# Second layer's output projection: where its weights are loaded, cast and split

## The chip, the cores and the metric

The kernel runs on one core of a Trainium2 chip. A core has five engines with an instruction queue each: TensorE (PE in the profile, its weight loads PEld), VectorE (DVE), ScalarE (ACT), GpSimd (POOL) and SyncE (SP), which here only starts transfers. Each engine takes its instructions strictly in the order in which the program put them; an instruction that waits for a semaphore holds up everything behind it on its engine. Sixteen DMA engines carry the transfers that SP and POOL start. The metric is the device time of one execution in microseconds, the median over several executions.

## The reference

Two pre-norm residual layers over 1024 tokens of width 1024, and a last RMS norm. The first layer is a gated linear recurrence, the second is causal attention with a forget gate, 16 heads of width 64. Of the second layer the change touches the last line alone, the product with `fox_w_out`.

```python
def fox_mixer(h, w_in, b_f, w_out):
    ...
        logits = jnp.einsum("bqhd,bkhd->bhqk", q_blk.astype(jnp.float32), kf) * scale
        logits = logits + (cq_blk[..., :, None] - ck[:, :, None, :])
        ...
        p = jax.nn.softmax(logits, axis=-1)
        return jnp.einsum("bhqk,bkhd->bqhd", p, vf)
    ...
    y = o * jax.nn.silu(gate)
    return y @ w_out.astype(h.dtype)
...
        x = x + fox_mixer(h, fox_w_in[j], fox_b_f[j], fox_w_out[j])
    return rms_norm(x, final_g)
```

## The kernel before

Everything is held feature-major: a tile is 128 features by 512 tokens, one half of the sequence. float32 products are made of three: an operand is split into a high part in the short format of TensorE and a low part, the rest, and high*high, low*high and high*low are added up. The high part of a weight is a cast on ACT (`to_hi`, a CAST `wh<-wf` in the rows), the low part a subtraction on DVE that needs the cast's result (`to_lo`, L110, `wl<-wf,wh`). A weight tile comes from HBM into a buffer `wf`, of which there are three, in turn; `fetch` (L65) starts the load on SP's queue.

The attention goes head by head. For a head `hd` and a half `c` of its queries, `maxima` (L941) makes the scores `S` on TensorE in blocks of 128 queries, a maximum over the masked scores on DVE (L965), the exponential `p` on ACT with its row sums, the reciprocal of the sums and the split probabilities `pp` (ACT, then DVE L979), and a transpose of these by DMA on SP's queue into `pT` (L982). `weigh` (L988) then multiplies `pT` with the values `V` into `O`, `gated` and `split_y` make the layer's result `y` of it.

`run` (L1038) weaves these together by a string of digits: each digit takes one step of `weigh` or `maxima`, each dot one step of `fill`, independent TensorE work. For the heads 12 to 15 `fill` ends in `partial` (L1104). It walks over 16 tiles (db, c), db of the 8 blocks of 128 output features, c of the two halves, in the order (0,0), (1,0), (0,1), (1,1), (2,0), (2,1), (3,0) ... (7,1). A tile adds 18 products (six pairs of heads, three products each) in a bank `ops1`, adds the residual `x` that POOL's queue brought (L1113, L1116), and for most tiles POOL's queue writes it back. "Tile n" below means block db = n; both halves use the same weights. The last two pairs of heads come later (`late`, weights `woh`, `wol`; `turned`, bank `turn`), and the output follows from there.

The weights of block db are made by `split_out(db)` (L1084), with six blocks of 128x128 in two loads, one of 128x512 (256 KB) and one of 128x256 (128 KB), two casts and two subtractions. `partial` calls it at the head of a tile, for the tile itself if that is still to do, and for the next block where `c if db < 2 else not c` holds. So the program text puts load, cast and split of block db+1 ahead of a tile's products: those of block 2 ahead of the products of (1,1), those of block 3 ahead of (2,0), and so on.

The text is not the final order: the framework's scheduler places each instruction on its engine by priority, which follows the text, and by when its operands are expected. `tc.issue_after(x)` gives what stands under it a priority behind the instruction x. `seen[0]` is the exponential that was written last.

Of the kernel before, what the change touches and what calls it, by code (L numbers as in the profile page):

```python
# [12 lines left out]
F32R = mybir.dt.float32r  # L13
# [6 lines left out]
P = 128  # L20
SEQ = 1024
HALF = 512
KT = 8
# [12 lines left out]
def f32(ap):  # L36
    return ap.bitcast(F32)
# [3 lines left out]
def trunk(ctx: ExitStack, tc: tile.TileContext, xt, w0, wg, wo0, pc, gn, gf, w1, wv, wf, bf, wo1, out):  # L41
    nc = tc.nc

    def pool(name, bufs, **kw):
        return tc.tile_pool(name=name, bufs=bufs, **kw)
# [4 lines left out]
    wpool = ctx.enter_context(pool("w", 4))  # L50
# [14 lines left out]
    def fetch(to, src):  # L65
        loaded_last[0] = loads_by[0].dma_start(to, src)

    def matmul(*args, **kw):
        pe[0] = nc.tensor.matmul(*args, **kw)  # L69
        return pe[0]  # L70
# [25 lines left out]
    def to_hi(hi, src, eng, scale=None):  # L96
        if eng is nc.scalar:
            if scale is None:
                cast_last[0] = nc.scalar.copy(hi, src)
            else:  # L100
                nc.scalar.activation(hi, src, AF.Copy, scale=scale)
        elif eng is nc.gpsimd:
            nc.gpsimd.tensor_scalar(hi, src, 1.0 if scale is None else scale, 0.0, ALU.mult, ALU.add)
        elif scale is None:
            eng.tensor_copy(hi, src)
        else:
            eng.tensor_scalar(hi, src, scale, None, ALU.mult)

    def to_lo(lo, src, hi, eng):
        return eng.tensor_tensor(lo, src, f32(hi), ALU.subtract)  # L110
# [3 lines left out]
    def loaded(shape):  # L114

        if spare and next(loads) % 4 == 3:
            return spare[0].tile([P, *shape], F32, tag="wx", name="wf")
        return wpool.tile([P, *shape], F32, tag="wf", name="wf", bufs=3)

    def split_weights(src, shape, hi_eng, lo_eng, parts=wpool):  # L120
        wt = loaded(shape)
        for part, sl in src:
            fetch(wt[:, :, sl], part)
        hi = parts.tile([P, *shape], F32R, tag="wh", name="wh")
        lo = parts.tile([P, *shape], F32R, tag="wl", name="wl")
        a, b, c = (t.rearrange("p a b -> p (a b)") for t in (wt, hi, lo))
        to_hi(b, a, hi_eng)
        to_lo(c, a, b, lo_eng)
        return [(hi[:, k], lo[:, k]) for k in range(shape[0])]

    def weights(src, parts=wpool, lo_eng=nc.gpsimd):

        for k in range(0, src.shape[1], 4):
            n = min(4, src.shape[1] - k)
            yield from split_weights([(src[:, k : k + n], slice(0, P))], (n, P), nc.scalar, lo_eng, parts)

    def gemm_steps(ps, pairs, chunks=(slice(0, HALF),)):

        pairs = list(pairs)
        for cs in chunks:  # L140
            o = ps[:, cs]
            for i, ((wh, wl), (xh, xl)) in enumerate(pairs):
                matmul(o, wh, xh[:, cs], start=i == 0, stop=False)
                matmul(o, wl, xh[:, cs], start=False, stop=False)
                matmul(o, wh, xl[:, cs], start=False, stop=i == len(pairs) - 1)
                if i % 2:
                    yield
# [51 lines left out]
    with nullcontext(ExitStack()) as l0:  # L199
# [45 lines left out]
        k = 0  # L245
# [138 lines left out]
        def out_weights(g, d0):  # L384

            wt = loaded([4, P])
            for j in range(2):
                nc.sync.dma_start(wt[:, 2 * j : 2 * j + 2], wo0[d0 + j, :, 2 * g : 2 * g + 2])
            hi = wpool.tile([P, 4, P], F32R, tag="wh", name="wh")
            lo = wpool.tile([P, 4, P], F32R, tag="wl", name="wl")  # L390
            to_hi(hi, wt, nc.scalar)
            to_lo(lo, wt, hi, nc.vector)
            return [[(hi[:, 2 * j + i], lo[:, 2 * j + i]) for i in range(2)] for j in range(2)]
# [184 lines left out]
        wl = [w for d0 in range(0, KT, 2) for w in out_weights(NB // 2 - 1, d0)]  # L578
# [41 lines left out]
    with ExitStack() as l1:  # L620
# [11 lines left out]
        seen = [None]  # L632
# [137 lines left out]
        wo = {}  # L770
# [306 lines left out]
        def beside(steps, first, more):  # L1077

            for i, _ in enumerate(steps):
                if i >= first:  # L1080
                    next(more, None)
                yield

        def split_out(db):  # L1084
            if db < KT and db not in wo:
                wo[db] = list(weights(wo1[db, :, :6], lo_eng=nc.vector))

        def first_out():
            split_out(0)
            yield from ()  # L1090
# [3 lines left out]
        def home(db):  # L1094

            if db == 4:
                two = at.tile([P, 2, HALF], F32, tag="sg", name="x3")
                homes[4], homes[3] = two[:, 0], two[:, 1]
            elif db == 5:
                four = tu.tile([P, 4, HALF], F32, tag="T0", name="x4")  # L1100
                homes.update(zip((2, 5, 6, 7), (four[:, i] for i in range(4))))
            return homes[db]

        def partial(todo):  # L1104

            for db, c in todo:
                split_out(db)
                if c if db < 2 else not c:
                    split_out(db + 1)

                kept = c == 0 and db > 3
                x = home(db) if kept else rpool.tile([P, HALF], F32, tag="R", name="xp")
                nc.gpsimd.dma_start(x, x1d[c, :, db])  # L1113
                pt = ps.tile([P, HALF], F32, tag="g", name="ops1")
                yield from gemm_steps(pt, zip(wo[db], [y1[c][pair] for pair in range(6)]))
                nc.vector.tensor_tensor(x, x, pt, ALU.add)  # L1116
                if not kept:
                    nc.gpsimd.dma_start(x1d[c, :, db], x)
# [135 lines left out]
        for hd in range(HEADS):  # L1254
            pair = hd // 2
            if hd % 2 == 0:
                if hd < 12:
                    fill = play(next(fills))
                elif hd == 12:
                    todo = [(db, c) for c in range(2) for db in range(2)]  # L1260
                    todo += [(db, c) for db in range(2, KT) for c in range(2)]
                    splits = [split_loaded(c) for c in range(2)]
                    fill = chain(
                        play(next(fills)),
                        play(last_g[0]),
                        high_y(0),
                        first_out(),
                        beside(play(last_g[1]), 1, splits[0]),
                        high_y(1),
                        beside(partial(todo), 3, splits[1]),  # L1270
                        last_gains(),
                        turned(0, 0),
                        turned(0, 1),
                    )
            elif pair < 6:
                fill = play(next(fills))
# [86 lines left out]
def build(arrays):  # L1363
    import concourse.bacc as bacc

    nc = bacc.Bacc("TRN2", target_bir_lowering=False, num_devices=1)
    args = [
        nc.dram_tensor(f"in_{k}", v.shape, mybir.dt.from_np(v.dtype), kind="ExternalInput").ap()
        for k, v in arrays.items()
    ]  # L1370
    args.append(nc.dram_tensor("out_t", (KT, P, SEQ), F32, kind="ExternalOutput").ap())
    with tile.TileContext(nc, schedule_with_timeline_sim=True) as tc:
        trunk(tc, *args)
    return nc
# [9 lines left out]
```

## Time and profile before

| | |
|---|---|
| three runs | 1059.81, 1063.55, 1062.22 us; median 1062.22 |
| the profiled execution, its own time | 1059.12 us |
| its span, first to last instruction | 1057.4 us |
| mean granted TensorE clock | 0.996 |
| DMA | 148.92 MB, of it 161937 of 219806 packets under 512 B |
| `wf<-in_wo` | 64 loads of 128 KB on average, SP's queue |

The heads 12 to 15, and with them `partial`, run from about 928 us (the first product of `ops1`) to 1018 us; the end of the program follows. A row of the timeline gives start, length, engine, line, operation, output<-input and form, and in brackets how long the engine was idle before it and what ended that. SPq is SP's queue; its rows give the time that starting a transfer took, not its arrival. The names in the rows have no buffer numbers.

### The profile page before, as it was taken

To read this page: it belongs to the slowest core of one execution; us is meant where nothing else is said; L and a number is where in the kernel's file an instruction comes from. 1 tells how busy PE (TensorE), PEld (TensorE's weight loads), DVE (VectorE), ACT (ScalarE), POOL (GpSimd) and SP (SyncE) were. 2 spreads that over 40 slices of the span, in tenths; PEclk is the share of its full clock that TensorE was granted. 3 is DMA by queue.
4 is the path that set the end of the run, shared out by engine and by line. 5 is a ranking of instruction groups with operands and counts; after the bars stand their busy time and mean duration, and the time that the engine had idled before them with its cause. 6 is when DMAs were issued, how large, how long until landed. Compare 5 with 4: busy or idle time off the path is not lost. (4 is left out here: it accounts for less than half of the span.)

```text
span 1057.4 us, 15071 instructions
## 1 busy us (share of the span) xinstructions
PE 1022.6 (97%) x5094; PEld 710.3 (67%) x5094; DVE 786.5 (74%) x1456; ACT 660.7 (62%) x1211; POOL 90.6 (9%) x87
## 2 busy tenths in 40 slices
PE   9999999999999999998999989999999999999997
PEld 6787878888888888765444456444754448477676
DVE  7789657667856868895879875888578875986575
ACT  8479666565657565567656755666466764854455
POOL 1311112012101120001000000000000000012100
PEclk9999999999999999999999999999999999999999
DMA  7112424233423311443688993898748985789984
GB/s 246 61 50 63 124 84 144 68 115 108 133 66 113 122 50 48 161 141 75 150 166 169 185 208 70 182 192 175 182 95 189 176 190 133 168 196 250 230 199 160
DMA packets 219806, 148.92 MB, mean 141 GB/s; under 512 B 161937, under 2 KB 174865, under 8 KB 219729
## 3 DMA queue, kind: packets, MB, share of 16 engines
q1 hardware_dynamic: 217328, 140.09, 54.0%
q0 software_dynamic: 2400, 7.87, 2.5%
q8 instruction: 40, 0.66, 0.2%
q14 instruction: 38, 0.30, 0.1%
HBM read 73.33 MB, written 11.67 MB: 80 GB/s over the span
## 5 line engine op out<-in xcount | busy, mean ns | idle before, releaser
L69 PE MATMUL gps<-h,w 128*128 128x512 f16 x1152 | 269.1, 380 | 1.3 <-DVE qkl L795 1.1
L69 PEld LDWEIGHTS <-w 128*128 128x128 f16 x1152 | 104.2, 98 | 126.8 <-issue 14.0
L57 ACT ACTIVATE p<-S,m 128x128 f32<-128x128 f32 (+7 forms) x128 | 94.4, 738 | 78.0 <-DVE m L965 32.4
L57 ACT ACTIVATE pp<-p,sums 128x128 f16<-128x128 f32 (+7 forms) x128 | 96.6, 770 | 34.9 <-DVE sums L977 22.0
L979 DVE SCALAR_TENSOR_TENSOR pp<-p,sums,pp 128x128 f16<-128x128 f32 (+7 forms) x128 | 102.5, 812 | 13.5 <-ACT pp L57 12.4
L69 PE MATMUL S<-T,U 96*128 96x512 f32 (+7 forms) x384 | 106.4, 386 | 5.2 <-ACT p L57 4.1
L965 DVE CUSTOM_DVE_ANT_0 S<-S,mask 128x128 f32<-128x128 f32 (+7 forms) x128 | 96.9, 758 | 11.8 <-PE S L69 10.5
L69 PE MATMUL vps<-w,h 128*128 128x256 f16 (+1 forms) x768 | 90.6, 280 | 11.4 <-ACT w L57 7.4
L110 POOL TENSOR_TENSOR wl<-wf,wh 128x512 fp32r<-128x512 f32 x46 | 69.3, 1511 | 324.5 <-ACT wh L57 268.5
L69 PEld LDWEIGHTS <-h 128*128 128x128 f16 x768 | 76.3, 100 | 25.9 <-issue 9.9
L69 PEld LDWEIGHTS S<-T,U 128*128 128x128 f32 (+1 forms) x384 | 66.9, 189 | 39.3 <-ACT p L57 19.1
L57 ACT CAST wh<-wf 128x512 fp32r<-128x512 f32 x88 | 51.6, 592 | 51.1 <-PE ops L69 27.6
L69 PE MATMUL ups<-hh,wh 128*128 128x512 f32 x192 | 76.2, 398 | 1.1 <-ACT hh L57 1.0
L69 PE MATMUL ops<-yh,wh 128*128 128x512 f32 x192 | 76.7, 399 | 0.6 <-ACT yh L57 0.6
L69 PE MATMUL ups<-hh,wl 128*128 128x512 f32 x192 | 75.7, 394 | 1.0 <-POOL wl L110 1.0
L69 PE MATMUL ups<-hl,wh 128*128 128x512 f32 x192 | 76.2, 397 | 0.2
L69 PE MATMUL ops<-yh,wl 128*128 128x512 f32 x192 | 75.7, 394 | 0.1
L69 PE MATMUL gps<-hh,wh 128*128 128x512 f32 x192 | 75.7, 394 | 0.1
L69 PE MATMUL gps<-hh,wl 128*128 128x512 f32 x192 | 75.5, 393 | 0.0
L69 PE MATMUL gps<-hl,wh 128*128 128x512 f32 x192 | 75.5, 393 | 0.0
L403 DVE TENSOR_TENSOR x<-x,ops 128x512 f32<-128x512 f32 x80 | 54.0, 679 | 28.2 <-PE ops L69 27.9
L69 PE MATMUL ops<-yl,wh 128*128 128x512 f32 x192 | 74.6, 394 | 0.0
(196 smaller groups left out, 1877.9 us busy)
## 6 DMA issues: line engine op xcount, KB each, us to landing
wf<-in_w SPq DMA_DIRECT2D x106, 256.0 KB
wsf<-in_w SPq DMA_DIRECT2D x48, 256.0 KB
wf<-in_wo SPq DMA_DIRECT2D x64, 128.0 KB
T<-qkh SPq DMA_DIRECT2D x64, 128.0 KB
U<-qkh SPq DMA_DIRECT2D x64, 128.0 KB
x<-in_xt SPq DMA_DIRECT2D x16, 256.0 KB
wsf<-in_wv SPq DMA_DIRECT2D x16, 256.0 KB
x1d<-x SPq DMA_DIRECT2D x16, 256.0 KB
```

Source lines behind the costliest of these rows:

```text
L57: act[0] = op(*args, **kw)
L69: pe[0] = nc.tensor.matmul(*args, **kw)
L110: return eng.tensor_tensor(lo, src, f32(hi), ALU.subtract)
L403: nc.vector.tensor_tensor(x, x, pt, ALU.add)
L965: nc.vector.tensor_tensor_reduce(S[:, :n], S[:, :n], mask[:, SEQ - n :], -1.0, -NEG, ALU.add, ALU.min, accum_out=m)
L979: nc.vector.scalar_tensor_tensor(both[:, :, 1], p, r, both[:, :, 0], ALU.mult, ALU.subtract)
```

## The change

Load and split come apart. A new `load_out(db)` starts the two loads of a block; `split_out` calls it and then only casts and subtracts. `partial` loads the next block ahead of a tile's products, as before, but casts and splits it behind them, under `issue_after` of the exponential that was written last.

```diff
+        raw_out = {}
+
+        def load_out(db):
+            if db < KT and db not in raw_out:
+                raw_out[db] = []
+                for k, n in ((0, 4), (4, 2)):
+                    wt = loaded((n, P))
+                    fetch(wt, wo1[db, :, k : k + n])
+                    raw_out[db].append(wt)
+
         def split_out(db):
+            load_out(db)
             if db < KT and db not in wo:
-                wo[db] = list(weights(wo1[db, :, :6], lo_eng=nc.vector))
+                wo[db] = []
+                for wt in raw_out[db]:
+                    hi, lo = (wpool.tile([P, *wt.shape[1:]], F32R, tag=t, name=t) for t in ("wh", "wl"))
+                    to_hi(hi, wt, nc.scalar)
+                    to_lo(lo, wt, hi, nc.vector)
+                    wo[db] += [(hi[:, k], lo[:, k]) for k in range(wt.shape[1])]
...
                 split_out(db)
-                if c if db < 2 else not c:
-                    split_out(db + 1)
+                ahead = c if db < 2 else not c
+                if ahead:
+                    load_out(db + 1)
...
                 yield from gemm_steps(pt, zip(wo[db], [y1[c][pair] for pair in range(6)]))
+                if ahead:
+                    with tc.issue_after(seen[0].ins):
+                        split_out(db + 1)
                 nc.vector.tensor_tensor(x, x, pt, ALU.add)
```

TensorE's order does not change at all. On the other engines it does from the middle of `partial` on. The numbers in the names belong to one build each: block 2 is `wh_9049`, `wh_9055` before and `wh_9104`, `wh_9108` now.

ACT, where head 13 turns to head 14; before:

```order
L57 ACTIVATE p_8987,sums_8644<-S_8980,m_8985 128x1024
L57 CAST wh_9049<-wf_9047 128x512
L57 ACTIVATE pp_8989<-p_8987,sums_8644 128x8x128
L57 CAST wh_9055<-wf_9053 128x256
L57 ACTIVATE yo_8622<-O_9012,wsq_238 64x512
L57 ACTIVATE p_9037,sums_9030<-S_9032,m_9035 128x128
L57 CAST wh_9116<-wf_9114 128x512
L57 ACTIVATE pp_9039<-p_9037,sums_9030 128x128
L57 ACTIVATE p_9083,sums_9030<-S_9078,m_9081 128x256
L57 ACTIVATE pp_9085<-p_9083,sums_9030 128x2x128
L57 ACTIVATE p_9104,sums_9030<-S_9099,m_9102 128x384
L57 ACTIVATE pp_9106<-p_9104,sums_9030 128x3x128
```

and now:

```order
L57 ACTIVATE p_8987,sums_8644<-S_8980,m_8985 128x1024
L57 ACTIVATE pp_8989<-p_8987,sums_8644 128x8x128
L57 ACTIVATE yo_8622<-O_9012,wsq_238 64x512
L57 ACTIVATE p_9037,sums_9030<-S_9032,m_9035 128x128
L57 ACTIVATE pp_9039<-p_9037,sums_9030 128x128
L57 ACTIVATE p_9075,sums_9030<-S_9070,m_9073 128x256
L57 ACTIVATE pp_9077<-p_9075,sums_9030 128x2x128
L57 ACTIVATE p_9096,sums_9030<-S_9091,m_9094 128x384
L57 CAST wh_9104<-wf_9047 128x512
L57 CAST wh_9108<-wf_9049 128x256
L57 ACTIVATE pp_9098<-p_9096,sums_9030 128x3x128
```

The casts of block 2 moved from behind the exponential of 128x1024 to behind that of 128x384; the cast of block 3 left this stretch for a later place.

DVE, the same place, now (before, no `wl` stands between these two additions):

```order
L1136 TENSOR_TENSOR xp_9051<-xp_9051,ops1_9053 128x512
L965 ISA S_9091,m_9094<-S_9091,mask_4069 128x384
L965 ISA m_9094 128x1
L979 SCALAR_TENSOR_TENSOR pp_9077<-p_9075,sums_9030,pp_9077 128x2x128
L976 TENSOR_SCALAR sums_9030<-sums_9030 128x1
L977 RECIPROCAL sums_9030<-sums_9030 128x1
L110 TENSOR_TENSOR wl_9105<-wf_9047,wh_9104 128x512
L110 TENSOR_TENSOR wl_9109<-wf_9049,wh_9108 128x256
L979 SCALAR_TENSOR_TENSOR pp_9098<-p_9096,sums_9030,pp_9098 128x3x128
L965 ISA S_9135,m_9138<-S_9135,mask_4069 128x512
L965 ISA m_9138 128x1
L1136 TENSOR_TENSOR xp_9118<-xp_9118,ops1_9120 128x512
```

The two subtractions of block 2 moved behind the reciprocal of the third block of scores; the first addition is that of (1,1), the last one that of (2,0).

SP's queue, where head 14's second half is transposed; before:

```order
L66 DMA x3_9335<-x1d_94 128x512
L982 DMA_TRANSPOSE pT_9238<-pp_9248 128x10x128
L66 DMA wf_9433<-in_wo1 128x512
L982 DMA_TRANSPOSE pT_9238<-pp_9286 128x12x128
L66 DMA wf_9439<-in_wo1 128x256
L66 DMA x0_9742<-x1d_94 128x512 x2
L66 DMA x4_9445<-x1d_94 128x512
L982 DMA_TRANSPOSE pT_9238<-pp_9315 128x14x128
L982 DMA_TRANSPOSE pT_9238<-pp_9359 128x16x128
L66 DMA wf_9454<-in_wo1 128x256 x2
```

and now:

```order
L66 DMA x3_9327<-x1d_94 128x512
L982 DMA_TRANSPOSE pT_9230<-pp_9240 128x10x128
L982 DMA_TRANSPOSE pT_9230<-pp_9286 128x12x128
L66 DMA x0_9742<-x1d_94 128x512 x2
L66 DMA x4_9437<-x1d_94 128x512
L982 DMA_TRANSPOSE pT_9230<-pp_9315 128x14x128
L982 DMA_TRANSPOSE pT_9230<-pp_9351 128x16x128
L66 DMA wf_9433<-in_wo1 128x512
L982 DMA_TRANSPOSE pT_9404<-pp_9412 128x2x128
L66 DMA wf_9435<-in_wo1 128x256
```

The two loads of block 6 (`wf_9433` and the 128x256 after it) moved from ahead of the transposes of 14 and 16 blocks to behind them.

## The prediction

> **What bounds the kernel now.** I read the page first, then the table of windows for the last two hundred microseconds, where the edited code runs, then who TensorE waited for there.
>
> ```profile
> span 1057.4 us, 15071 instructions
> PE 1022.6 (97%) x5094; PEld 710.3 (67%) x5094; DVE 786.5 (74%) x1456; ACT 660.7 (62%) x1211; POOL 90.6 (9%) x87
> ...
> 940.00:960.00 20.00, 20.00 (x94) 15.18 (x93) 15.06 (x37) 10.66 (x22) 3.41 (x7) 1.00 1.01 218
> 960.00:980.00 20.00, 20.00 (x96) 15.17 (x95) 13.94 (x30) 11.03 (x18) 5.59 (x11) 1.00 1.01 270
> 980.00:1000.00 20.00, 17.80 (x81) 12.88 (x80) 11.10 (x30) 7.76 (x18) 1.35 (x3) 1.00 1.05 225
> 1000.00:1020.00 20.00, 20.00 (x100) 15.05 (x100) 15.51 (x31) 10.68 (x18) 2.91 (x6) 1.00 0.99 224
> ...
> PE O L69 <- DMA pT<-pp: 2.1, 1, 2.1
> ...
> 1036.40 14.88 PE turn L69 x86
> ```
>
> The columns of a window are its length, then busy time of PE, weight loads, VectorE (DVE), ScalarE (ACT) and GpSimd, the granted clock, the busy share of the DMA engines, and GB/s. TensorE is busy in every microsecond from 940 to 1020 but for 2.2, and one wait of 2.1 us, on transposed probabilities, makes up nearly all of that. The DMA engines are full as well (share 1.01, 1.01, 1.05, 0.99). ACT and DVE are half to three quarters busy. The last row is the end of the chain of waits: it closes with 86 products of TensorE in a row. So a microsecond of TensorE idling in this stretch is a microsecond of the kernel, and the most that the stretch has to give back is about 2.1 us. TensorE's order is the same before and after, product for product; what can move is when its operands are ready.
>
> **The change part by part.** Nothing is added or removed on any engine: the same casts, the same subtractions, the same loads, in other places.
>
> *Tile 2's weights.* Today they are cast early, long before use. The rows in the timeline (start, length, engine):
>
> ```profile
> 942.39 0.62 ACT L57 CAST wh<-wf 128x512 fp32r<-128x512 f32 x1 [0.27 <-PE ops L69]
> 943.04 0.69 DVE L110 TENSOR_TENSOR wl<-wf,wh 128x512 fp32r<-128x512 f32 x1 [0.53 <-ACT wh L57]
> ...
> 949.45 0.51 PE L69 MATMUL S<-T,U 128*128 128x384 f32 x2
> 949.65 0.69 DVE L1116 TENSOR_TENSOR xp<-xp,ops 128x512 f32<-128x512 f32 x1
> 949.80 0.39 PE L69 MATMUL ops<-yhh,wh 128*128 128x512 f32 x1
> 950.03 0.40 PE L69 MATMUL ops<-yhh,wl 128*128 128x512 f32 x1
> ...
> 950.33 0.55 DVE L965 CUSTOM_DVE_ANT_0 S<-S,mask 128x384 f32<-128x384 f32 x1
> ...
> 950.97 0.58 ACT L57 ACTIVATE p<-S,m 128x384 f32<-128x384 f32 x1
> ```
>
> The products of tile 2, half 0, begin at 949.80 (high part) and 950.03 (low part). In the new order the cast stands on ACT directly behind the exponential of 128x384. That exponential cannot run sooner: it waits for the mask-and-maximum on DVE (950.33), which waits for the scores that TensorE issues at 949.45 and for the addition of tile 1 (949.65), which TensorE itself releases. At best it gains the 0.1 us by which the reciprocal no longer stands ahead of the maximum. So: exponential from 950.87 to 951.45, cast 0.62 to 952.07, subtraction 0.69 to 952.76, and with some hundredths for the hand-overs (943.04 follows the end of the cast at 943.01) the low-part product starts at 952.8 instead of 950.03: **+2.8 us**. In between one high-part product runs at about 952.1. It cannot be less than 2.5, since the chain has no spare link; at most it is about 3.3, if the split probabilities that now stand ahead of the subtraction on DVE hold it up by the half microsecond that such a row takes (0.55 for the maximum above). The second pair of parts (128x256) follows in time, because twelve products stand ahead of their use. Behind the waiting product on TensorE stand the 128x512 scores, so maximum, exponential and transposes of this head all come 2.8 us later too; nothing catches up, since TensorE has no idle time to shorten before 992.
>
> *Tiles 3, 4, 5 and 7.* Their casts also stand behind an exponential, but with more products between it and the use.
>
> ```profile
> 954.08 0.69 ACT L57 ACTIVATE p<-S,m 128x512 f32<-128x512 f32 x1 [1.35 <-DVE m L965]
> 959.30 0.58 PE L69 MATMUL ops<-yhh,wh 128*128 128x512 f32 x1
> ...
> 976.88 1.12 ACT L57 ACTIVATE p<-S,m 128x1024 f32<-128x1024 f32 x1 [0.98 <-DVE m L965]
> 982.39 0.40 PE L69 MATMUL ops<-yhh,wh 128*128 128x512 f32 x1
> ```
>
> Tile 3 has 959.30 - 954.77 = 4.5 us for a cast and a subtraction of 1.3 us, tile 5 has 4.4 us. Tile 4 lies alike, and tile 7's cast keeps its place behind those of the late weights. I cost these at nothing; the products in between are the cover, and without it each would cost its 1.3 us.
>
> *Tile 6's loads.* On SP's queue the two loads of tile 6 (256 and 128 KB) move from ahead of the two largest transposes of head 14 to behind them, while the transposes' place against the x loads stays.
>
> ```profile
> 973.91 1.73 SPq L66 DMA_DIRECT2D wf<-in_wo  x1
> ...
> 978.37 0.56 SPq L66 DMA_DIRECT2D wf<-in_wo  x1
> ...
> 980.49 11.96 SPq L982 DMA_TRANSPOSE pT<-pp  x2
> 992.54 1.48 SPq L66 DMA_DIRECT2D wf<-in_wo  x3
> ...
> 994.47 0.61 PE L69 MATMUL O<-pT,v 128*128 128x512 f16 x2 [2.09 <-DMA pT<-pp]
> 994.72 0.58 PE L69 MATMUL ops<-yhh,wh 128*128 128x512 f32 x1
> 995.14 0.39 PE L69 MATMUL ops<-yhh,wl 128*128 128x512 f32 x1
> ...
> 996.26 0.62 ACT L57 CAST woh<-wf 128x512 fp32r<-128x512 f32 x1 [2.80 <-DMA wf<-in_wo]
> ...
> 985.00:990.00 5.00, 4.89 (x22) 3.73 (x21) 3.93 (x15) 3.06 (x10) 0.00 (x0) 1.00 1.16 270
> ```
>
> Times are in the old frame, before the 2.8. The gain: 384 KB less ahead of the transposes is 393 KB / 270 GB/s = 1.5 us, so the wait of 2.09 shrinks to about 0.6. The loss: the load is now issued when the issue of the transposes ends, at 992.45 - 1.5 = 990.95. The next load in today's queue went out at 992.54 and its cast began at 996.26, 3.7 us later; so tile 6's cast begins at about 994.7, its high part is ready at 995.3, its low part at 996.0, where TensorE wants it at 995.14. Net **+0.9 us**. Bounds: -2.1, if the weights come in time and the whole wait goes; +2.3, if the transposes gain nothing (992.45 + 3.7 + 0.6 + 0.7 = 997.45 against 995.14). I take 0.9, since the load rests on a measured issue-to-cast time out of the same jam. The subtraction that waits there on DVE has the maximum of the 128x512 scores behind it, whose exponential runs at 996.78 today, itself behind a cast that waits for a load; so that chain loses about nothing.
>
> *The clock.* TensorE waits over 2 us four times in this trace, and after two of them the granted clock fell to half:
>
> ```profile
> 622.30 4.88 PE L69 MATMUL vps<-w,h 128*128 128x256 f16 x30 [2.84 <-ACT w L57]
> 618.40:621.80 3.40, 1.06 (x11) 0.46 (x9) 1.88 (x3) 1.66 (x4) 0.00 (x0) 1.00 0.65 190
> 621.90:625.20 3.30, 2.90 (x14) 2.01 (x14) 2.25 (x3) 1.79 (x3) 0.00 (x0) 0.50 1.13 199
> 747.04 2.74 PE L69 MATMUL vps<-w,h 128*128 128x256 f16 x17 [2.39 <-ACT w L57]
> 744.70:748.10 3.40, 1.06 (x10) 0.95 (x10) 1.74 (x3) 1.63 (x4) 0.00 (x0) 1.00 1.04 261
> 748.20:751.50 3.30, 3.30 (x18) 2.32 (x17) 1.39 (x2) 0.77 (x2) 0.00 (x0) 0.50 0.97 195
> 872.22 2.02 PE L69 MATMUL vps<-w,h 128*128 128x256 f16 x17 [2.17 <-ACT w L57]
> 990.60:993.90 3.30, 1.78 (x8) 1.12 (x6) 0.71 (x3) 0.61 (x1) 0.54 (x1) 1.00 1.36 189
> ```
>
> A stretch of 3.4 us in which TensorE was busy for only 1.06 is followed by one of 3.4 us at 0.50; with 1.78 busy (the wait before 994.47) it is not. The two longer waits dropped the clock, the two shorter ones (2.17 and 2.09) did not. Half the clock for 3.4 us loses 1.7 us of products. The two falls lie 126.3 us apart, 37 stretches of 3.41 us (by that division); the same steps from 748.2 give a stretch from about 949.6 to 953.0, which would hold the new wait at tile 2 whole, with 0.8 us of busy time in it. Where these stretches lie against the program I cannot know for another execution; a wait of 2.8 us can straddle two. Bounds: 0 to 1.7 for each of the two waits, tile 2 and tile 6. I take one fall, **+1.7 us**.
>
> The Trainium skill, page "TensorE: Matmul & The Clock Gate", section "Part 1: The HAM clock gate (the "warmup" mystery)", says that the clock falls back after an idle window of about 3.4 us. By that rule a wait of 2.8 us would leave the clock whole and the sum would lose its 1.7; this trace, where waits of 2.84 and 2.39 us were followed by half the clock, speaks against it.
>
> Sum: 2.8 + 0.9 + 1.7 = 5.4 us. The profiled execution took 1059.12, which becomes 1064.5. It lies 3.1 us under the median of the three runs, and the same 5.4 on the median of 1062.22 gives **1067.6**. What a measurement of this kernel can tell from no change is about 0.3%, 3.2 us.
>
> **The rivals.**
>
> *No fall of the clock.* Both waits straddle their stretches: 2.8 + 0.9 = 3.7, so 1065.9. For it: two waits of four left the clock whole. Against it: the new wait is as long as the longest, 2.84. It is also what that page of the Trainium skill gives. Chance 0.25; of it I count two thirds as slower by more than 3.2.
>
> *The queue pays for it.* The two loads out of the way free the transposes in full, tile 6's weights still come in time because everything before came 2.8 us later, and the clock stays: 2.8 - 2.1 = 0.7, so 1062.9, no change. It decides from the point where, in the old frame, the transposes have landed by 992.4 and tile 6's subtraction is done by 995.1. For it: the DMA engines are the scarce thing there (share 1.16 in 985 to 990), so what leaves the queue is felt. Against: the load must wait for the transposes' issue, and then took 3.7 us to its cast. Chance 0.20.
>
> *Everything lands badly.* Transposes gain nothing, both waits halve the clock: 2.8 + 2.3 + 3.4 = 8.5, so 1070.7. Chance 0.17.
>
> *Faster.* The one mechanism on that side is the emptier front of ACT and DVE: if the chain from scores to exponential at 949 to 951 ran 2.8 us sooner, tile 2 would not wait and only the gain of 2.1 at the transposes stayed: 1060.1. It decides from the point where the exponential of 128x384 ends by 948.7. The row against it is the first of the scores, 949.45, which TensorE issues in the same order as before. Even then it gains less than 3.2. Chance 0.03, with its size doubled by luck.
>
> The forecast has 0.35. Slower: 0.35 + 0.17 + two thirds of 0.25 = 0.69; no change: 0.20 + 0.08 = 0.28; faster 0.03. The range reaches from "the queue pays" (1062.9, rounded up to 1063.0) to "everything lands badly" (1070.7): 1063.0 to 1070.7, with the 2 in 10 for what lies outside either end.
>
> **What would show it.** Right: TensorE waits before tile 2's first product, for the cast, and again before its second, for the subtraction, 2.8 us in all; a window at 0.50 in the PEclk column within 4 us of it; before the weighted sum of head 14 the wait on the transposes falls to under 1 us and a wait for tile 6's cast stands behind it. Wrong: tile 2 starts within 0.5 us of the products ahead of it (then the chain had a spare link); the wait on the transposes stays 2 us or more (then the loads were never what delayed them); tile 3, 4, 5 or 7 waits for a cast (then my cover was misread).

## The result, and the profile after

The change makes the kernel slower, by about twice what was forecast.

| | before | with the change |
|---|---|---|
| time, median (range, runs) | 1062.54 us (1059.81 to 1063.55, 4) | 1074.62 us (1070.77 to 1075.54, 4) |
| ratio to before, 95% interval | | 1.0097 [1.0067, 1.0126] |
| the profiled execution: time, span | 1059.12, 1057.4 us | 1075.39, 1073.6 us |
| first product of `ops1` | 928.6 us | 934.3 us |

By the ratio that is +10.3 us (0.0097 x 1062.5); +5.4 was forecast, and the median lies above the range of 1063.0 to 1070.7. The two spans differ by more, 16.2 us, and one row of each shows why. The view groups the high-part products of `partial`, with the start of the first and the last of them; before, then the change:

```profile
L69 PE MATMUL ops<-yhh,wh x96: 387/395/582, 928.6 to 1017.5; 128*128 128x512 f32 x96
```

```profile
L69 PE MATMUL ops<-yhh,wh x96: 387/395/796, 934.3 to 1034.1; 128*128 128x512 f32 x96
```

Ahead of 928.6 the two programs have one order on every engine, so the 5.7 us by which the second starts later belong to that execution (a second trace of the change, experiment 7, starts at 930.0). From the first to the last of these products, below called **the stretch**, it was 88.9 us and is 99.8: +10.9, and this agrees with the ratio. The waits of TensorE from 925 to 1045 (us in total, times, longest) of the change say where, beside the 2.1 us of before:

```profile
PE O L69 <- DMA pT<-pp: 6.2, 1, 6.2
PE ops L69 <- ACT wh L57: 2.6, 2, 2.2
PE ops L69 <- DVE wl L110: 0.2, 1, 0.2
```

The timeline of TensorE, at tile 2 and at the weighted sum of head 14:

```profile
957.92 0.50 PE L69 MATMUL ops<-yhh,wh 128*128 128x512 f32 x1 [2.20 <-ACT wh L57]
958.64 0.64 PE L69 MATMUL ops<-yhh,wl 128*128 128x512 f32 x1 [0.23 <-DVE wl L110]
...
1008.40 1.03 PE L69 MATMUL O<-pT,v 128*128 128x512 f16 x2 [6.17 <-DMA pT<-pp]
1009.83 0.80 PE L69 MATMUL ops<-yhh,wh 128*128 128x512 f32 x1 [0.39 <-ACT wh L57]
```

The wait for block 2 is there as forecast, first for the cast, then for the subtraction. The wait on the transposes was to shrink from 2.09 to 0.6 and has tripled; tile 6's cast costs only 0.39 behind it. The windows of the change (columns as in the prediction) show both falls of the clock, the second twice as long as the first, and something about the DMA engines:

```profile
955.50:958.80 3.30, 0.87 (x4) 0.35 (x3) 2.71 (x8) 2.50 (x6) 0.00 (x0) 1.00 1.18 157
958.90:962.20 3.30, 3.30 (x9) 2.53 (x9) 0.55 (x2) 0.00 (x0) 1.07 (x2) 0.50 1.15 179
995.00:1000.00 5.00, 5.00 (x24) 4.14 (x23) 1.14 (x6) 1.64 (x5) 0.00 (x0) 1.00 1.18 111
1000.00:1005.00 5.00, 2.23 (x10) 1.49 (x8) 1.14 (x3) 0.00 (x0) 0.00 (x0) 1.00 1.13 109
1006.70:1010.00 3.30, 1.21 (x3) 0.31 (x3) 0.20 (x1) 0.84 (x2) 0.54 (x1) 0.50 1.13 296
1010.00:1013.40 3.40, 3.40 (x8) 2.39 (x9) 3.12 (x9) 2.55 (x6) 0.00 (x0) 0.50 0.75 203
```

From 995 to 1005 the DMA engines are full (1.18, 1.13) and move 110 GB/s; with the same share they moved 270 in the window 985 to 990 of before. What runs there stands on two queues. POOL's queue, before and then with the change, and SP's queue with the change:

```profile
975.81 1.06 POOL L1113 DMA_DIRECT2D x<-x1d  x2 [2.49 <-PE S L69]
979.21 0.54 POOL L1113 DMA_DIRECT2D xp<-x1d  x1 [2.33 <-DMA x1d<-xp]
979.74 0.54 POOL L1113 DMA_DIRECT2D x<-x1d  x1
```

```profile
987.79 0.54 POOL L1130 DMA_DIRECT2D xp<-x1d  x1 [5.00 <-DMA x1d<-xp]
988.48 1.59 POOL L1130 DMA_DIRECT2D x<-x1d  x3
```

```profile
988.14 16.40 SPq L982 DMA_TRANSPOSE pT<-pp  x2
1004.60 0.57 SPq L66 DMA_DIRECT2D wf<-in_wo  x1
```

The three `x` loads of tiles 5, 6 and 7 (256 KB each) stood on POOL's queue ahead of and around the `xp` load of tile (5,1); now all three stand behind it. Before, the transposes of 14 and 16 blocks started at 980.49, 0.75 us behind the last of the three; now they start at 988.14, 0.34 us ahead of the first. Issuing the two transposes took SP 11.96 us and takes 16.40. The table of DMA issues gives the median time from issue to landing of these three loads, before (970 to 996) and now (980 to 1010):

```profile
x<-x1d POOLq DMA_DIRECT2D x3, 256.0 KB, 7.8
```

```profile
x<-x1d POOLq DMA_DIRECT2D x3, 256.0 KB, 15.2
```

Loads and transposes got slow together. That is the theory the experiments test, **A**: two costs, (1) block 2's wait with its fall of the clock, (2) POOL's x loads and SP's transposes in flight side by side. They overlap before too, since a load took 7.8 us to land; what the experiments have to show is which meeting is the costly one.

### The profile page after: what moved, and what is told of

The parts are those of the page before. It is cut to its first block, busy times and chain, and to the rows that moved or that the text cites. A ratio compares the mean times of both kernels' runs of the same rounds, so it can differ in the third digit from the quotient of the medians.

```text
span 1073.6 us, 15067 instructions
## 1 busy us (share of the span) xinstructions
PE 1028.1 (96%) x5094; PEld 713.2 (66%) x5094; DVE 784.9 (73%) x1456; ACT 660.7 (62%) x1211; POOL 92.5 (9%) x87
```

## The experiments

Medians are set beside runs of before on the same chips; "stretch" is first to last high-part product of `ops1` in the one trace, as above (88.9 before, 99.8 with the change).

| experiment | median us | ratio to before, 95% interval | stretch us | wait before `O` us |
|---|---|---|---|---|
| 1 change, block 2 split ahead | 1069.21 | 1.0073 [1.0046, 1.0099] | 98.3 | 8.0 |
| 2 before, block 2 split late | 1062.58 | 1.0017 [1.0000, 1.0033] | 92.1 | 0.7 |
| 3 change, x loads of 6, 7 held | 1067.31 | 1.0062 [1.0036, 1.0089] | 90.5 | 0 |
| 4 before, x loads of 6, 7 later | 1060.78 | 0.9987 [0.9966, 1.0007] | 91.8 | 2.9 |
| 5 before, x loads with the 14-block transpose | 1067.85 | 1.0073 [1.0046, 1.0099] | 97.0 | 8.4 |
| 6 change, x loads on SP's queue | 1063.02 | 1.0033 [1.0011, 1.0056] | 92.1 | none named |
| 7 the change again | 1070.29 | 1.0106 [1.0076, 1.0136] | 102.1 | 8.3 |
| 8 experiment 3 again | 1069.59 | one run | 96.7 | 4.4 |
| 9 change, both cures | 1063.81 | 1.0029 [1.0010, 1.0048] | 88.6 | 0.4 |
| 10 before, block 2 split one exponential sooner | 1061.94 | 1.0003 [0.9982, 1.0024] | 89.7 | 1.1 |
| 11 before, x loads on SP's queue | 1058.80 | 0.9978 [0.9960, 0.9996] | 87.9 | 0.3 |
| 12 before, x loads all ahead | 1061.88 | 1.0023 [1.0000, 1.0046] | 89.9 | none named |

### 1. The change, with block 2 split ahead

```diff
                 if ahead:
                     load_out(db + 1)
+                if db == 1:
+                    split_out(db + c)
```

> The change, with cast and split of block 2 alone put back ahead of the products of (1,1); the rest of the change stays, and POOL's order too (the three x loads of tiles 5, 6 and 7 behind the xp load of (5,1)). Theory A (two separate costs: the wait for block 2 with its fall of the clock, and transposes of head 14 that share the DMA engines with POOL's x loads): the wait of 2.4 us at tile 2 and the half clock behind it go, 2.6 + 1.7 = 4.3 us; the wait on the transposes stays near 6 us: 1074.6 - 4.3 = 1070.3. Rival (the second wait follows from the first, because the 2.6 us shift what meets on the DMA engines): the wait on the transposes falls to about 2 us too, about 1064.

1069.21, as A has it (four of the six times lie from 1068.9 to 1070.4, two at 1063.05 and 1064.84). The wait at tile 2 is gone and the one on the transposes stays, so the second does not follow from the first. Waits from 925 to 1045:

```profile
PE O L69 <- DMA pT<-pp: 8.0, 1, 8.0
PE ops L69 <- ACT wh L57: 0.3, 1, 0.3
```

### 2. Before, with block 2 alone split late

As an edit of the change (the other blocks are split ahead again):

```diff
                 if ahead:
                     load_out(db + 1)
+                if ahead and db != 1:
+                    split_out(db + 1)
```

> The kernel before, with cast and split of block 2 alone put behind the products of (1,1). POOL's order is that of before. Theory A: the wait at tile 2 (2.6 us) and half the clock for 3.4 us (1.7, if the wait fills one stretch), the wait on the transposes of head 14 stays at or under 2.5 us: 1062.5 + 2.6 to 4.3 = 1065.1 to 1066.8. Rival (the second wait follows from the first): the wait on the transposes grows to about 6 us: 1071 to 1073.

```profile
PE ops L69 <- ACT wh L57: 2.2, 1, 2.2
PE O L69 <- DMA pT<-pp: 0.7, 1, 0.7
...
PE ops L69 <- DVE wl L110: 0.2, 1, 0.2
```

Block 2's wait has the size it has in the change, and POOL's order and the transposes are those of before. The stretch grows by 3.2 us, the time by 1.8 (0.0017 x 1060.9, the median of before beside it), with an interval from 0 to 3.5. Both are less than the 4.5 us lost at tile 2: the 2.1 us wait on the transposes is where products that come later lose less, and 0.7 is left of it in the trace. The rival (a wait of 6 us) fell.

### 3 and 8. The change, with x loads of tiles 6 and 7 held

```diff
+                if kept and db == 6:
+                    nc.gpsimd.tensor_scalar(x[:1, :1], pT[1][:1, 0, 0, HALF - 1 :], 1.0, 0.0, ALU.mult, ALU.add)
+                    nc.gpsimd.tensor_scalar(home(7)[:1, :1], pT[1][:1, 0, 0, HALF - 1 :], 1.0, 0.0, ALU.mult, ALU.add)
+                    nc.gpsimd.dma_start(x, x1d[c, :, db])
+                    nc.gpsimd.dma_start(home(7), x1d[c, :, 7])
+                elif not kept or db < 6:
                     nc.gpsimd.dma_start(x, x1d[c, :, db])
```

The element that is copied comes from the 16-block transpose, and the load overwrites it.

> The change, with POOL's x loads of tiles 6 and 7 held until the transpose of 16 blocks of head 14 has landed (by a copy of one element from pT into each x buffer, which the load then overwrites). Theory A (the x loads share the DMA engines with the transposes and slow both): the wait on the transposes falls from 6.2 to 2.5 us or less and the half clock behind it goes: 1074.6 - 3.7 - 1.4 = about 1069.5. Rival B (the transposes cost that time by themselves, once they start earlier): the wait stays near 6 us, 1074 to 1075.

The trace agreed, no wait on the transposes at all; the median, 1067.31, agreed only by half, and the ten times lay apart: three from 1060 to 1062, seven from 1066 to 1071. So it ran once more for a trace:

> The third experiment once more (the change with POOL's x loads of tiles 6 and 7 held until the 16-block transpose has landed): its ten times lay in two groups, 1060 to 1062 and 1066 to 1071, and the trace came from the first. Theory A: a trace of the second group, if it is one, shows a long wait on the transposes while the writes and the remaining x load of POOL's queue run among them; of the first group, no wait there. Rival: the second group has its time from somewhere ahead of the first product of ops1, and the stretch is the same in both.

This one was of the second group, 1069.59, with the stretch at 96.7 in place of 90.5. One x load, tile 5's, was not held. POOL's and SP's rows of the first trace:

```profile
981.13 0.54 POOL L1136 DMA_DIRECT2D x<-x1d  x1
```

```profile
981.23 3.49 SPq L982 DMA_TRANSPOSE pT<-pp  x1
```

and of the second, with its wait:

```profile
985.86 0.54 POOL L1136 DMA_DIRECT2D x<-x1d  x1
```

```profile
985.42 2.89 SPq L982 DMA_TRANSPOSE pT<-pp  x1
```

```profile
PE O L69 <- DMA pT<-pp: 5.0, 2, 4.4
```

In the good execution this load starts 0.1 us ahead of the 14-block transpose, in the bad one 0.44 us behind it. Of the 9.2 us between the two executions 6.2 lie in the stretch and 3.5 ahead of it (it starts at 927.1 and at 930.6), so the rival of the eighth run, the same stretch in both, fell, though a part of the difference does lie ahead. Two traces do not prove that the order within half a microsecond decides, but the other traces agree with it. Where an x load of POOL's queue starts 0.34 to 1.15 us behind the 14-block transpose (the change twice, experiments 1, 5 and 8), TensorE waits 4.4 to 8.4 us; where the last one starts 0.1 to 1.5 us ahead of it (before, experiments 2, 3 and 10), 0 to 2.1. (This edit also moved tile 6's weight loads between the two transposes, so it is not a clean test of the held loads alone.)

### 4. Before, with two x loads later

```diff
+                if not kept or db < 6:
                     nc.gpsimd.dma_start(x, x1d[c, :, db])
+                if (db, c) == (5, 1):
+                    for d in (6, 7):
+                        nc.gpsimd.tensor_scalar(home(d)[:1, :1], x[:1, :1], 1.0, 0.0, ALU.mult, ALU.add)
+                        nc.gpsimd.dma_start(home(d), x1d[0, :, d])
```

Here `x` is the buffer of the `xp` load of (5,1), so both loads wait for its landing.

> The kernel before, with POOL's x loads of tiles 6 and 7 put later, behind the landing of the xp load of (5,1), so that they run among the transposes of 14 and 16 blocks; nothing else is moved. Theory A: the wait on the transposes grows from 2.1 to between 4 and 6 us, with a fall of the clock when over about 2.3: 1062.5 + 2 to 5.5 = 1064.5 to 1068. Rival B: the wait stays at 2 us, 1062.5.

A miss for A as it was put: 1060.78, no slower than before. The rows: POOL's issue, then two windows.

```profile
984.79 1.12 POOL L1118 DMA_DIRECT2D x<-x1d  x2
```

```profile
987.00:989.00 2.00, 2.00 (x10) 1.65 (x9) 1.71 (x8) 1.47 (x6) 0.00 (x0) 1.00 1.09 330
989.00:995.00 6.00, 3.27 (x15) 2.31 (x13) 1.96 (x7) 1.07 (x3) 0.00 (x0) 0.94 1.24 165
```

The two loads are issued 3.2 us behind the 14-block transpose (981.62) and while they move, the engines run at 330 GB/s: no jam; behind them, beside a write of POOL's queue and the 16-block transpose, 165. So the loads do not hurt merely by coming later than before; but here there are two of them behind the transpose and not three, and the wait is 2.9 us. Experiment 5 starts them with the transpose, as the change does.

### 5. Before, with the x loads together with the 14-block transpose

```diff
+                if not (kept and db > 4):
                     nc.gpsimd.dma_start(x, x1d[c, :, db])
+                elif db == 5:
+                    for d in (5, 6, 7):
+                        nc.gpsimd.tensor_scalar(homes[d][:1, :1], pps[6][:1, 0, 1, :1], 1.0, 0.0, ALU.mult, ALU.add)
+                    for d in (5, 6, 7):
+                        nc.gpsimd.dma_start(homes[d], x1d[0, :, d])
```

`pps[6]` is the tile of probabilities that the 14-block transpose reads.

> The kernel before; POOL's three x loads of tiles 5, 6 and 7 stand behind the xp load of (5,1) as in the change, and start when the probabilities of the 14-block transpose are ready (three one-element operations on POOL that read them), so together with that transpose. TensorE, DVE and ACT have the order of before, SP too up to the 16-block transpose; tile 6's weights are loaded early as before. Theory A (x loads on POOL's queue and the transposes on SP's slow each other, in whatever kernel): the wait on the transposes grows from 2.1 to 6 or 8 us as in the change and in the first experiment, with a fall of the clock behind it: 1061 + 4 to 8 = 1065 to 1069. Rival B (the place of tile 6's loads on SP's queue is what matters): the wait stays near 2 us, 1061.

This is the run that decides. TensorE, DVE, ACT and, up to the transposes, SP stand as before; only POOL's rows have the order of the change (and three one-element operations more). 1067.85, and a wait of 8.4 us. POOL, SP, the wait, and the engines meanwhile:

```profile
984.57 1.65 POOL L1120 DMA_DIRECT2D x<-x1d  x3
```

```profile
984.22 17.12 SPq L983 DMA_TRANSPOSE pT<-pp  x2
```

```profile
PE O L69 <- DMA pT<-pp: 8.4, 1, 8.4
```

```profile
990.00:995.00 5.00, 4.92 (x22) 3.67 (x20) 0.00 (x0) 0.93 (x3) 0.00 (x0) 1.00 1.20 128
995.00:1000.00 5.00, 0.00 (x0) 0.00 (x0) 1.99 (x6) 0.00 (x0) 0.00 (x0) 0.82 1.29 107
```

Full engines at 107 to 128 GB/s again. Rival B, tile 6's place on SP's queue, fell: that place was not touched.

### 6. The change, with the x loads on SP's queue

```diff
-                nc.gpsimd.dma_start(x, x1d[c, :, db])
+                (nc.sync if kept and db > 4 else nc.gpsimd).dma_start(x, x1d[c, :, db])
```

> The change, with the x loads of tiles 5, 6 and 7 on SP's queue, where they stand between the 12-block and the 14-block transposes, in place of POOL's queue. Theory A (it is the two queues side by side that make both slow): in one queue nothing overlaps; the three loads of 256 KB take about 3 us at 270 GB/s ahead of the transposes, the wait on these falls from 6.2 to about 2: about 1069. Rival B: the transposes still take 16 us from issue to landing, plus the 3 us that now stand ahead of them: 1075 or more.

1063.02, better than A expected. The same 768 KB stand ahead of the transposes in their own queue, and no wait on the transposes is named any more. SP's queue:

```profile
982.52 1.48 SPq L1130 DMA_DIRECT2D x<-x1d  x3
984.09 0.86 SPq L66 DMA_DIRECT2D x<-x1d  x2
985.04 9.86 SPq L982 DMA_TRANSPOSE pT<-pp  x2
```

9.86 us of issuing in place of 16.40. On SP's queue the loads also go out ahead of the 14-block transpose, in time and not only in the queue. So this run does not tell which of the two cures: the queue, or the order.

### 7. The change again

> The change once more, unaltered, for its time beside the same runs of before as the others and for a second trace of the stretch. Theory A (a matter of order, so of every execution): the wait on the transposes is 5 us or more again, 1071 to 1074. Rival C (chance: the first trace was an unlucky execution): a wait of 3 us or less, and a time that spreads down to 1066.

1.0106, and the wait on the transposes, 8.3 us, is longer still: not chance, so rival C fell.

### 9. The change with both cures

The edits of 1 and 6 together.

> The change with both cures: cast and split of block 2 back ahead of the products of (1,1), and the x loads of tiles 5, 6 and 7 on SP's queue. What is left of the change is the late split of blocks 3 to 7 and their later loads. Theory A (two costs, block 2's wait and the two queues side by side, and no third): no wait at tile 2, none over 2.5 us on the transposes, 1059 to 1062 beside 1060.8 for before. Rival (the late splits or tile 6's late loads have a price of their own): a wait on a cast of 1 us or more at tiles 3 to 7, 1063 or more.

```profile
PE ops L69 <- ACT wh L57: 1.2, 1, 1.2
...
PE O L69 <- DMA pT<-pp: 0.4, 1, 0.4
PE ops L69 <- DVE wl L110: 0.2, 1, 0.2
```

The stretch is back at 88.6 in the trace; the median, 1063.81, is 0.29% over before and above what A allowed. The rival has a part: with the jam gone, tile 6 waits 1.4 us for its late weights, while the wait on the transposes is 1.7 shorter than before (2.1 to 0.4). In this execution, one of the two fastest of ten (1061.18), the two cancel; where the other 3 us of the median come from the one trace does not show, and it was not tried further. Nor do the times show block 2's cure here: experiment 6, where block 2 is split late, has 1.0033 and this one 1.0029, though the stretches of their traces are 92.1 and 88.6.

### 10. Block 2 one exponential sooner

The edit of 2, with the split of block 2 written behind the third step of the products of (1,1), so that its casts follow the exponential of 128x256.

> The kernel before with cast and split of block 2 behind the exponential of 128x256, one exponential sooner than in the change. From the rows of before this exponential ends at 949.42 with its sums read, the cast at 950.05, the subtraction at 950.8, where TensorE wants them at 949.80 and 950.03: waits of 0.3 and 0.5 us, 0.8 in all. Theory A (half of the cost of block 2's late split is the clock, which a short wait leaves whole): tile (2,1) comes 0.8 us later than before and the clock stays at 1.00: 1061.6. Rival (the clock falls behind any wait there, or the cost is in the order of the casts): 2.5 to 4.5 us later at (2,1), 1063 to 1065.

```profile
PE ops L69 <- DVE wl L110: 1.1, 1, 1.1
```

```profile
953.00:956.40 3.40, 2.31 (x11) 1.81 (x11) 2.71 (x9) 1.93 (x5) 0.00 (x0) 1.00 1.11 181
956.40:959.80 3.40, 3.40 (x16) 2.79 (x15) 0.89 (x2) 0.45 (x2) 1.07 (x2) 1.00 1.13 247
```

One wait of 1.1 us where 0.8 was expected (tile (2,1) starts 27.4 us behind (0,0), in place of 25.9), the clock whole behind it, and a time like before's (1.0003). The rival fell. Beyond its idle time the wait costs 0.5 us here and 2.1 of 4.5 us in the change, so about 1.6 of these go with the clock, near the 1.7 of the prediction's working.

### 11 and 12. Towards a faster kernel

The edit of 6 on the kernel before:

> The kernel before with the x loads of tiles 5, 6 and 7 on SP's queue instead of POOL's. Theory A: the last of these loads can no longer run beside the transposes of head 14; the wait of 2.1 us on them shrinks, by 0 to 2: 1059 to 1061 beside 1060.8. Rival (in one queue the 256 KB loads stand ahead of the transposes and delay them as much): 1061 to 1063.

And the three x loads written together at the head of (5,0), which moves one row on POOL's queue:

> The kernel before with one row moved on POOL's queue: the third x load ahead of the xp load of (5,1), so that all three are issued 3 us or more ahead of the 14-block transpose. Every other engine and queue has the order of before. Theory A: the wait on the transposes is 2 us or less: 1059.5 to 1061 beside 1060.8. Rival (the place of the x loads ahead of the transposes does not matter): no difference, a wait of 2 to 3 us.

The eleventh has no wait on the transposes worth the name (0.28 us before `O`) and a median of 1058.80: ratio 0.9978 [0.9960, 0.9996], a little faster than before and the best of all.

The twelfth is a miss in its time: no wait on the transposes either, though the x loads stay on POOL's queue, but 1.0023. With the loads 6 us and more ahead of the 14-block transpose the wait goes as it does on SP's queue; so the order alone can cure it, and no run here shows that the queue matters. The loads now delay others. A load of `wf` lands late, ACT waits for it, the exponential behind comes late, and TensorE waits for that (ACT's row, then TensorE's):

```profile
987.93 0.62 ACT L57 CAST wh<-wf 128x512 fp32r<-128x512 f32 x1 [3.46 <-DMA wf<-in_wo]
```

```profile
991.60 0.66 PE L69 MATMUL S<-T,U 128*128 128x384 f32 x2 [1.98 <-ACT p L57]
```

## Why the prediction was wrong, point by point

**Tile 2's wait: right.** Forecast +2.8 for the delay by cast and subtraction, and +1.7 for the clock, 4.5 together. That the sum comes out to a hundredth is luck. The starts of the first product of tile (0,0) and of (2,1), before and with the change:

```profile
928.58 0.40 PE L69 MATMUL ops<-yhh,wh 128*128 128x512 f32 x1
...
954.45 0.39 PE L69 MATMUL ops<-yhh,wh 128*128 128x512 f32 x1
```

```profile
934.34 0.40 PE L69 MATMUL ops<-yhh,wh 128*128 128x512 f32 x1
...
964.71 0.39 PE L69 MATMUL ops<-yhh,wh 128*128 128x512 f32 x1
```

25.87 and 30.37 us: +4.50, of it 2.43 idle. The first low-part product starts 0.72 us behind the first high-part one in place of 0.23, so with the wait of 2.20 ahead of the pair it came 2.7 us late, where the prediction has 2.8. Where the prediction erred a little was "nothing catches up": in experiment 2 the later wait on the transposes took back 1.4.

**Tiles 3, 4, 5, 7 at nothing: right** in the change; no wait there is named.

**Tile 6: the step that failed.** "The gain: 384 KB less ahead of the transposes is 393 KB / 270 GB/s = 1.5 us, so the wait of 2.09 shrinks to about 0.6." The wait grew to 6.17. Two things were missing. The prediction compared SP's queue before and after and not POOL's, where the change moved two rows: the x loads behind the `xp` load, and with that behind the start of the 14-block transpose. And it took 270 GB/s as a rate that the engines keep whatever they carry; with x loads beside the transposes it was 110. Even the dearer of its two bounds, "if the transposes gain nothing", had no room for a loss.

The gain itself is not shown either. In experiment 9, with POOL's loads out of the way and tile 6's loads behind the transposes, the wait on these is 0.4; but in experiment 11, where tile 6's 384 KB still stand ahead of them, it is 0.3, and in experiment 12 none. So, by these traces, what made the wait of 2.09 was the x loads and not tile 6's weights, as the prediction's own sign of being wrong has it ("then the loads were never what delayed them"). The loss is real: tile 6 waits 1.4 us for cast and subtraction in experiment 9 (2.4 forecast).

**The clock.** One fall was taken, two came. The second begins within the 6.17 us wait, at 1006.6, and lasts 6.8 us, two of the prediction's stretches of 3.41. In this part of the program, in the traces of the change and the experiments, every wait of 2.2 us or more, 12 of 12, went with such a fall, within it or behind it; six of them are the wait of 2.20 at tile 2. But that is no rule for the length of a wait: from 600 to 900 us in the same 14 traces 11 of 32 waits of 2.2 to 3.0 us left the clock whole. One is in the trace of the change itself, a wait of 2.39 us that ends at 748.69:

```profile
747.20:750.60 3.40, 1.91 (x18) 1.71 (x18) 1.84 (x4) 2.17 (x3) 0.00 (x0) 1.00 1.05 253
```

The prediction's fixed stretches of 3.41 us, called steps from here on, fit both. In each of the 14 traces the falls start whole numbers of 3.413 us apart (in the change at 624.3, 876.9, 958.9 and 1006.6: 74, 24 and 14 steps), and what goes with a fall is how long TensorE was busy within one such step. Of the steps at full clock from 600 us to the end of the stretch, every one with less than 1.35 us of work was followed by half the clock, none with more than 1.8 was, and between these it went both ways. The step that holds the 2.39 us wait has 1.91 of work, the one at tile 2 has 0.97 (955.4 to 958.8). So whether a wait of 2.2 to 3 us costs the fall depends on where the steps lie, and the chance of 0.25 for "no fall of the clock" was fair; that it fell at tile 2 in six traces of six is in part luck. The Trainium skill's page "TensorE: Matmul & The Clock Gate", section "Part 1: The HAM clock gate (the "warmup" mystery)", says that the clock falls back after an idle window of about 3.4 us. Here the window need not be wholly idle: 0.97 us of work in it was too little.

**The sum.** Of the 10.9 us of stretch, 4.5 are lost at tile 2, 4.1 on the transposes (6.17 - 2.09) and 0.4 at tile 6's cast. In the second fall TensorE was busy for 4.6 us (1.21 and 3.40), and half of that, 2.3, is lost by the prediction's working. That makes 11.3; the change takes 0.4 less than before between the first products of (2,1) and (5,1) (32.7 against 33.1), which leaves the 10.9. "Everything lands badly" (1070.7) came nearest, with its two falls of the clock, of which the second was longer still; but it has the transposes gain nothing, where they lost 4.1. By the times, POOL's order is the larger part: alone it costs 0.73% (experiment 5, 7.7 us), block 2's late split alone 0.17% (experiment 2, 1.8 us, with 0 in its interval).

What stays open: why the framework's scheduler put the `xp` load ahead of the x loads, and why a transpose suffers from loads that start within about a microsecond behind it, and not, or much less, from loads that start ahead of it or 3 us behind.

## What to carry to other kernels

When a change moves work on one engine, compare the order of every queue that starts transfers, also the ones that the diff does not mention: here ACT and DVE were edited, and most of the loss came from two rows on POOL's queue. A transfer that shares the DMA engines with a large DMA transpose is not priced by bytes over a rate; look which starts first, and try the loads ahead of the transpose, in its own queue for instance (experiments 6 and 11). A cast that feeds TensorE should not stand behind an exponential that waits for TensorE's own scores. A stall of 2 to 3 us can cost nearly double when half the clock follows; in a forecast that is a chance, two in three by the waits counted above, and not a certainty.

## What the runs showed of the hardware

Beside DMA transposes on SP's queue, 256 KB loads on POOL's queue that start 0.34 to 1.15 us behind the first of them, the engines move 107 to 128 GB/s though full, for about 10 us (the change, experiments 1, 5 and 7); with the x loads ahead in the transposes' queue, in experiment 11, they moved 281 to 329:

```profile
980.00:985.00 5.00, 5.00 (x27) 3.60 (x26) 3.48 (x7) 3.03 (x5) 0.54 (x1) 1.00 1.15 281
985.00:990.00 5.00, 5.00 (x24) 4.18 (x24) 4.47 (x16) 2.70 (x9) 0.54 (x1) 1.00 1.44 329
```

The Trainium skill, page "DMA: Bandwidth & Descriptors", section "Issuing engines are not separate DMA queues", says that transfers from all issuing engines run on the same 16 DMA engines and interleave, and that issuing from several saves only issue time. The runs agree that they share, at a busy share of 1.0 to 1.3, and add that sharing with a transpose can cost more than half of the rate: 110 GB/s against 270.

Up to the end of `partial` the clock fell to half for whole steps of 3.413 us, one to four of them, and the length of a wait alone did not decide it. It fell behind a wait of 1.98 us in experiment 12 (step from 988.6 to 992.0, 1.43 us of work in it). It stayed whole behind one of 2.09 before (step from 990.5, 1.86 us of work) and behind one of 2.95 in experiment 7, which ends at 873.6 and lies across the border of two steps: 2.01 us of work in the first, 1.86 in the second.
